# One layer on one core: row sums of w_ada in PSUM, sums at the replacements on VectorE, retention's banks dealt anew, remainders of the weights last

## The chip, the cores and the metric

The kernel runs on one core of one Trainium2 chip. The metric is the device time of one execution in microseconds. A product of two matrices runs on TensorE (PE in the profile), which reads SBUF and writes PSUM. VectorE (DVE), ScalarE (ACT) and GpSimd (POOL) do the elementwise work, and SyncE (SP) issues nearly all DMAs, in the order in which they stand in its queue.

## The reference

One decoder layer with two mixers side by side, 1024 positions, width 2048, 8 + 8 heads of 128:

```python
mod = jax.nn.silu(c) @ w_ada[layer] + b_ada[layer]
shift, scale, gate = jnp.split(mod, 3, axis=-1)
h = rms_norm(x, norm_gain[layer]) * (1.0 + scale[:, None, :]) + shift[:, None, :]
proj = h @ w_in[layer]                                  # 2048 x 8192
...
oa = merge_heads(stick_breaking_attention(qa, ka, split_heads(v_sb, SB_HEADS)))
oa = oa * jax.nn.silu(z_sb.astype(jnp.float32))
...
ob = head_group_norm(chunkwise_retention(qr, kr, vr), ret_norm_gain[layer])
ob = ob * jax.nn.silu(z_r.astype(jnp.float32))
y = jnp.concatenate([oa, ob], axis=-1).astype(x.dtype) @ w_out[layer]
x = x + (gate[:, None, :] * y).astype(x.dtype)
```

All of it is in float32. `w_ada` is 2048 x 6144; only one row vector, silu(c), is multiplied with it.

## The kernel before

**Products.** The two big projections are done by Strassen's scheme in Winograd's form: a *group* yields 256 output columns over half of the inner dimension by seven products (P1 to P7) in place of eight. A product is four pieces of the inner dimension (j = 0 to 3) by three matmuls of 128 x 512: the left operand (the activations: seven combinations A11, S2, S3, A12, S1, A22, S4, each in four tiles) and the weights are each split into a rounded part and a remainder, and hi x hi, hi x lo and lo x hi are added. In the profile `A_h`, `S_h` are left parts, `A_l`, `S_l` their remainders, `wh` the rounded weights (ScalarE, L259), `wl` their remainders (VectorE, L264). `mm3` (L150 to L152) issues the three matmuls of one j one after the other, so a product needs its `wl` with its third matmul. Four *sums* of raw weights for each group (T1 to T4, `make`, L254) run on GpSimd. Results leave PSUM by ScalarE (L286) and VectorE (L292, and L294 with the gate).

**Stages.** 80 groups run in one fixed row on TensorE, 560 products: a (16 groups, named e), b (32, f and g), c (16, h), y (8) and o (8). `plan` lays out at which product and which j each load, sum and split is issued; `run` issues the products. Beside them run tasks that are advanced one step with each *tick*; a tick is one j of a product, three matmuls. All engines' orders are written out by this one loop.

**Replacements.** At the end of a, b, c and y the left operand is replaced, one combination after the other, as soon as its last product is issued: `place` makes the rounded part on ScalarE (L146) and the remainder (L147) on VectorE for j = 0 to 2 and on GpSimd for j = 3. At most one tile is placed in two ticks. At a's end the new left comes from SBUF and GpSimd forms S2 and S4 of it (L682, L685); at the others each tile is loaded from DRAM first (`keep`, `mix`), into one of a few spare tiles (`ld`, `room(5)` lets the first four loads go only while five are spare).

**Beside a**: `second_half` multiplies w_ada's other half: 8 sums, each of 16 tiles of 256 KB with one factor per partition, added up in an SBUF tile (`acc`). For sums 0 to 3 VectorE does all (`weigh`, L436); for 4 to 7 it does half, and ScalarE scales the others (L635), which GpSimd adds (L637). One tile is consumed in two and three ticks in turn; four tiles (`ada_b`) are kept, and the load of the next waits for the oldest (L605, L608). `over_partitions` then sums over partitions by small matmuls (L414), four for each accumulator. `keep_left` also runs there, on GpSimd (L663).

**Beside b and c**: the stick-breaking heads (`sb_heads`: 12 steps per head, `SB_GAP` = 7 ticks apart: `scores` zp, sigmoids, a scan on VectorE, transposes tp, values oT) and then, beside c and y, the retention heads (`ret_heads`: ktp, sp, up, otp). Their PSUM tiles share the banks A0, A1, B and C.

Of the kernel before, what the change touches and what calls it, by code (L numbers as in the profile page):

```python
# [11 lines left out]
F32 = mybir.dt.float32  # L12
# [5 lines left out]
P = 128  # L18
# [11 lines left out]
NP = 4  # L30
# [29 lines left out]
def layer_kernel(ctx, tc, x, c, w_ada, b_ada, norm_gain, w_in, sb_q_gain, sb_k_gain, ret_norm_gain, w_out,  # L60
# [88 lines left out]
    def mm3(o, a_hi, a_lo, b_hi, b_lo, first, last):  # L149
        nc.tensor.matmul(o, a_hi, b_hi, start=first, stop=False, skip_group_check=True)  # L150
        nc.tensor.matmul(o, a_hi, b_lo, start=False, stop=False, skip_group_check=True)  # L151
        nc.tensor.matmul(o, a_lo, b_hi, start=False, stop=last, skip_group_check=True)  # L152
# [81 lines left out]
    class Group:  # L234
# [14 lines left out]
        def make(self, n):  # L249
# [4 lines left out]
            nc.gpsimd.tensor_tensor(t[o], t[a], t[b], op=op)  # L254
# [50 lines left out]
    def plan(groups):  # L305
# [7 lines left out]
        for k, (g, p) in enumerate(flat):  # L313
            g.at[p] = k
        for k, (g, p) in enumerate(flat):
            if p == "P1":
                on(k - 7, 0, lambda g=g: g.load(0))
                on(k - 6, 1, lambda g=g: g.load(1))
                on(k - 3, 1, lambda g=g: g.make("T3"))
                alone = g.at["P6"] == k + 1  # L320
                on(k - 2 if alone else k - 1, 3 if alone else 1, lambda g=g: g.make("T2"))
                on(g.at["P5"] - 3, 0, lambda g=g: g.make("T1"))
                on(max(g.at["P4"] - 4, g.at["P2"] - 1), 1, lambda g=g: g.make("T4"))
# [36 lines left out]
    def run(ks):  # L360

        for k in ks:
# [183 lines left out]
    plan(groups_a + groups_b + groups_c + groups_y + groups_o)  # L546
# [47 lines left out]
    def second_half():  # L594

        order_ = [(i, r) for i in range(8) for r in range(16)]
        src, accs_ = {}, {}
# [12 lines left out]
        def close(i):  # L610
            mod = ps.tile([P, 4], F32, tag="C", name=f"mod_b{i}")
            over_partitions(mod, accs_.pop(i))
# [12 lines left out]
        for n, (i, r) in enumerate(order_):  # L625
            if r == 0:
                accs_[i] = [k1b.tile([P, HALF], F32, tag="acc", bufs=2, name=f"acc_b{i}")]
            t = src.pop((i, r))
            if i < 4 or r % 2 == 0:
                weigh(accs_[i][0], t, r, r == 0)  # L630
            elif r == 1:
                accs_[i].append(k1b.tile([P, HALF], F32, tag="acc2", bufs=2, name=f"acc2_b{i}"))
                nc.scalar.activation(accs_[i][1], t, AF.Copy, scale=silu_c[:, r:r + 1])
            else:
                nc.scalar.activation(t, t, AF.Copy, scale=silu_c[:, r:r + 1])  # L635
                a2 = accs_[i][1]
                at(2, lambda a2=a2, t=t: nc.gpsimd.tensor_tensor(a2, a2, t, op=ALU.add))  # L637
            if r == 15:
                at(10, lambda i=i: close(i))
# [31 lines left out]
    def gather(n):  # L671
# [304 lines left out]
    def sb_heads():  # L976
        vts = {}
        for n in range(NS * NH + TURN + 2):
# [21 lines left out]
            if h < NH:  # L1000
# [6 lines left out]
                if nxt < NH and {f"n{nxt}", f"q{nxt}", f"k{nxt}", f"v{nxt}", f"z{nxt}"} <= ready:  # L1007
# [11 lines left out]
                    elif s == 11 and nxt in early:  # L1019
# [3 lines left out]
                        yield SB_GAP - 2  # L1023
                        continue
            if s == 3 and h < NH:
# [5 lines left out]
                yield SB_GAP - 6  # L1031
# [25 lines left out]
    def ret_heads():  # L1057
# [4 lines left out]
        for h in range(NH):  # L1062
# [47 lines left out]
            def scores_r(g):  # L1110
                sp = ps.tile([P, 4, P], F32, tag=("B", "A1")[g], name=f"sp_{h}_{g}")
# [8 lines left out]
            def values_r(g):  # L1120
# [40 lines left out]
            def finish(g, on, z):  # L1161
                tp = ps.tile([P, HALF], F32, tag=("B", "A0")[g], name=f"otp_{h}_{g}")
# [70 lines left out]
    def take(src, needs=()):  # L1233
# [7 lines left out]
        def tell(n):  # L1241
# [9 lines left out]
            for j in range(NP):  # L1251

                def do(j=j):
                    t = coming.pop((n, j))
                    place(n, j, t, nc.gpsimd if j == 3 else nc.vector)
# [111 lines left out]
```

## Time and profile before

| | |
|---|---|
| median of 3 runs | 2044.01 us (2043.52 to 2044.23) |
| the profiled execution: its own time | 2045.0 us |
| the profiled execution: its span | 2043.1 us |
| mean granted TensorE clock | 0.982 |
| PE busy | 1949.2 us, 95% |
| DVE, ACT, POOL busy | 1414.5 us, 882.9 us, 737.3 us |
| read and written in HBM | 278.51 MB and 108.10 MB, 189 GB/s |

The span runs from the first to the last instruction of the program; 1.9 us of the execution's own time lie around it. Matmuls overlap one another, so the busy time of PE also covers small gaps; what PE loses is seen better in the distances between starts.

### The profile page before, as it was taken

How to read it: one execution, taken by the hardware profiler on the slowest of the kernel's cores; microseconds unless marked ns; L12 is line 12 of the kernel's file. 1: busy time of each engine (PE TensorE's matmuls, PEld its weight loads, DVE VectorE, ACT ScalarE, POOL GpSimd, SP SyncE). 2: the span in 40 equal slices, each digit the busy share in tenths (PEclk: the TensorE clock that was granted, in tenths of full speed). 3: DMA queues.
4: the chain of work that ended last, by engine and by line, in shares of the span. 5: the costliest groups of instructions: out<-in, count | busy, mean ns of one | idle time of the engine just before them, and what ended most of it. 6: DMA issues, size and time to landing. Idle time of an engine off the chain costs nothing. (4 is left out here: it accounts for less than half of the span.)

```text
span 2043.1 us, 26981 instructions
## 1 busy us (share of the span) xinstructions
PE 1949.2 (95%) x9089; PEld 1561.3 (76%) x9089; DVE 1414.5 (69%) x2218; ACT 882.9 (43%) x1598; POOL 737.3 (36%) x507
## 2 busy tenths in 40 slices
PE   5879998998999999999999999899999999999998
PEld 4357777875777777788888888677888887887887
DVE  6668877647557676676666655778787886458655
ACT  4443244454344544545444454544343444345221
POOL 0434478665222223122322322545343444144221
PEclk9879999998999999999999999999999998999999
DMA  9737876633454455443434533867677787457665
GB/s 295 241 114 250 265 261 231 206 98 114 151 189 144 131 171 171 145 139 119 162 104 132 167 107 108 272 212 263 223 245 247 256 290 243 144 165 253 200 203 168
DMA packets 287326, 388.42 MB, mean 190 GB/s; under 512 B 32106, under 2 KB 164276, under 8 KB 287188
## 3 DMA queue, kind: packets, MB, share of 16 engines
q1 hardware_dynamic: 286784, 386.65, 58.5%
q8 instruction: 72, 1.18, 0.2%
q14 instruction: 66, 0.54, 0.1%
q10 hardware_dynamic: 404, 0.05, 0.0%
HBM read 278.51 MB, written 108.10 MB: 189 GB/s over the span
## 5 line engine op out<-in xcount | busy, mean ns | idle before, releaser
L254 POOL TENSOR_TENSOR wr_e<-wr_e,wr_e 128x512 f32<-128x512 f32 x240 | 351.0, 1476 | 746.4 <-DVE wl_e_P L264 679.2
L264 DVE TENSOR_TENSOR wl_e_P<-wr_e,wh_e_P 128x512 fp32r<-128x512 f32 x560 | 494.7, 884 | 119.4 <-ACT wh_e_P L259 119.2
L259 ACT ACTIVATE wh_e_P<-wr_e 128x512 fp32r<-128x512 f32 x560 | 352.0, 630 | 461.7 <-PE b_o L151 56.6
L254 POOL TENSOR_TENSOR wr_e<-wr_e 128x512 f32<-128x512 f32 x80 | 109.4, 1367 | 256.1 <-DVE wl_e_P L264 236.5
L917 DVE TENSOR_TENSOR_SCAN om<-om 128x128 f32<-128x128 f32 (+2 forms) x96 | 111.6, 1163 | 43.7 <-ACT om L908 41.4
L436 DVE SCALAR_TENSOR_TENSOR acc_b<-ada_b,silu_c,acc_b 128x512 f32<-128x512 f32 x88 | 97.9, 1113 | 31.4 <-DMA ada_b<-in_w_ada_dram 30.8
L292 DVE TENSOR_TENSOR pt<-b_f,pt 128x512 f32<-128x512 f32 x64 | 43.9, 687 | 69.3 <-PE b_f L152 69.2
L152 PE MATMUL b_e<-S_h,wl_e_P 128*128 128x512 f32 x192 | 78.7, 410 | 8.9 <-DVE wl_e_P L264 8.7
L150 PE MATMUL b_e<-S_h,wh_e_P 128*128 128x512 f32 x192 | 78.1, 407 | 5.7 <-ACT pt L286 5.7
L908 ACT ACTIVATE om<-zp,rq 128x128 f32<-128x128 f32 (+2 forms) x96 | 56.0, 584 | 61.6 <-PE zp L903 54.0
L151 PE MATMUL b_h<-S_l,wh_e_P 128*128 128x512 f32 x192 | 75.3, 392 | 3.4 <-DVE S_l L147 1.8
L151 PE MATMUL b_e<-S_l,wh_e_P 128*128 128x512 f32 x192 | 77.4, 403 | 0.0
L150 PE MATMUL b_h<-S_h,wh_e_P 128*128 128x512 f32 x192 | 76.7, 400 | 0.5 <-ACT S_h L146 0.5
L964 PE MATMUL oT<-a,v 128*128 128x256 f32 x320 | 76.8, 379 | 0.0
L150 PE MATMUL b_f<-S_h,wh_e_P 128*128 128x512 f32 x192 | 76.5, 399 | 0.0
L152 PE MATMUL b_h<-S_h,wl_e_P 128*128 128x512 f32 x192 | 75.4, 393 | 0.8 <-DVE wl_e_P L264 0.7
L150 PE MATMUL b_g<-S_h,wh_e_P 128*128 128x512 f32 x192 | 75.8, 395 | 0.0
L923 DVE TENSOR_TENSOR be<-be,om 128x127 f32<-128x127 f32 (+2 forms) x96 | 69.9, 728 | 8.0 <-DVE om L917 0.5
L151 PE MATMUL b_f<-S_l,wh_e_P 128*128 128x512 f32 x192 | 75.2, 392 | 0.0
L152 PE MATMUL b_g<-S_h,wl_e_P 128*128 128x512 f32 x192 | 74.9, 390 | 0.0
L152 PE MATMUL b_f<-S_h,wl_e_P 128*128 128x512 f32 x192 | 74.9, 390 | 0.0
L151 PE MATMUL b_g<-S_l,wh_e_P 128*128 128x512 f32 x192 | 74.9, 390 | 0.0
(401 smaller groups left out, 5325.2 us busy)
## 6 DMA issues: line engine op xcount, KB each, us to landing
wr_e<-in_w_in_dram SPq DMA_DIRECT2D x128, 512.0 KB
ada_b<-in_w_ada_dram SPq DMA_DIRECT2D x128, 256.0 KB
part<-pt SPq DMA_DIRECT2D x128, 256.0 KB
pt<-part SPq DMA_DIRECT2D x128, 256.0 KB
fin<-pt SPq DMA_DIRECT2D x128, 256.0 KB
ada_a<-in_w_ada_dram SPq DMA_DIRECT2D x64, 256.0 KB
wr_e<-in_w_out_dram SPq DMA_DIRECT2D x32, 512.0 KB
ld<-fin SPq DMA_DIRECT2D x54, 256.0 KB
```

The source lines that it names most:

```text
L150: nc.tensor.matmul(o, a_hi, b_hi, start=first, stop=False, skip_group_check=True)
L151: nc.tensor.matmul(o, a_hi, b_lo, start=False, stop=False, skip_group_check=True)
L152: nc.tensor.matmul(o, a_lo, b_hi, start=False, stop=last, skip_group_check=True)
L254: nc.gpsimd.tensor_tensor(t[o], t[a], t[b], op=op)
L259: nc.scalar.activation(hi, self.t[RIGHT[p]], AF.Copy)
L264: nc.vector.tensor_tensor(lo, self.t[RIGHT[p]], self.parts[p].bitcast(F32), op=ALU.subtract)
L292: nc.vector.tensor_tensor(t, src, t, op=ALU.add)
L436: nc.vector.scalar_tensor_tensor(acc, src, cj, acc, op0=ALU.mult, op1=ALU.add)
L908: nc.scalar.activation(om[:, :n], zp[:, :n], AF.Sigmoid, scale=rq[:, h, 1, i:i + 1])
L917: nc.vector.tensor_tensor_scan(rev, rev, rev, init, op0=ALU.mult, op1=ALU.bypass)
L923: nc.vector.tensor_tensor(be[:, :m], be[:, :m], om[:, 1:m + 1], op=ALU.mult)
L964: nc.tensor.matmul(ob, v[:, j, :], a[:, cl], start=diag and ib == 0 and b == 0 and j2 == 0, stop=ch == 0 and ib == 2, skip_group_check=True)
```

## The change

Five things, in the order of the file.

- The twelve matmuls of a product are issued by a table in place of `mm3`. `LATE`: first all four j with the rounded weights (hi, then the left's remainder), then all four with the weights' remainder. `FRESH`, for the first product with a combination that has just been placed: j = 0 and 1 in that manner, then j = 2 and 3 as before. The very first product keeps the old order.
- In the stretches around the ends of a, b, c and y (from the last group's P1 to four products behind its P3) the sums T1 to T4 run on VectorE in place of GpSimd.
- `place` uses VectorE for j = 3 too.
- `second_half`: VectorE does all 128 `weigh`s. The accumulator is a PSUM bank (A0 and A1 in turn), copied to SBUF by ScalarE at the end; there is one accumulator for each sum, so the modulation has four small matmuls in all 8 cases.
- Tasks: the gap behind two of the twelve steps of a stick-breaking head is 2 ticks longer. In retention five PSUM tiles get other banks, and both `normal`s stand one tick earlier.

```diff
-    def mm3(o, a_hi, a_lo, b_hi, b_lo, first, last):
-        nc.tensor.matmul(o, a_hi, b_hi, start=first, stop=False, skip_group_check=True)
-        nc.tensor.matmul(o, a_hi, b_lo, start=False, stop=False, skip_group_check=True)
-        nc.tensor.matmul(o, a_lo, b_hi, start=False, stop=last, skip_group_check=True)
+    PARTS = ((0, 0), (0, 1), (1, 0))
+    LATE = [(j, w, x) for j in range(NP) for w, x in PARTS[:2]] + [(j, 1, 0) for j in range(NP)]
+    FRESH = [(j, w, x) for j in (0, 1) for w, x in PARTS[:2]] + [(0, 1, 0), (1, 1, 0)] + \
+        [(j, w, x) for j in (2, 3) for w, x in PARTS]
+    PLAIN = [(j, w, x) for j in range(NP) for w, x in PARTS]
+    fresh = set()
...
         left[n, j] = hi, lo
+        fresh.add(n)
...
-            nc.gpsimd.tensor_tensor(t[o], t[a], t[b], op=op)
+            eng.tensor_tensor(t[o], t[a], t[b], op=op)
...
+        crowded = set()
+        def sum_of(g, n, k, j):
+            on(k, j, lambda: g.make(n, nc.vector if k in crowded else nc.gpsimd))
...
+        for g in lasts:
+            crowded |= set(range(g.at["P1"], g.at["P3"] + 5))
...
-            hi, lo = g.parts.pop(p)
+            o, w, n = getattr(g, into), g.parts.pop(p), LEFT[p]
+            order = PLAIN if not k else FRESH if n in fresh else LATE
+            fresh.discard(n)
             for j in range(NP):
-                a_hi, a_lo = left[LEFT[p], j]
-                mm3(getattr(g, into), hi[:, j, :], lo[:, j, :], a_hi, a_lo, p in ("P1", "P7", "P2") and j == 0,
-                    j == NP - 1)
+                for i in range(3 * j, 3 * j + 3):
+                    q, wi, xi = order[i]
+                    nc.tensor.matmul(o, w[wi][:, q, :], left[n, q][xi], start=p in ("P1", "P7", "P2") and i == 0,
+                                     stop=i == 11, skip_group_check=True)
...
             if r == 0:
-                accs_[i] = [k1b.tile([P, HALF], F32, tag="acc", bufs=2, name=f"acc_b{i}")]
-            t = src.pop((i, r))
-            if i < 4 or r % 2 == 0:
-                weigh(accs_[i][0], t, r, r == 0)
-            elif r == 1:
...
-            else:
-                nc.scalar.activation(t, t, AF.Copy, scale=silu_c[:, r:r + 1])
-                a2 = accs_[i][1]
-                at(2, lambda a2=a2, t=t: nc.gpsimd.tensor_tensor(a2, a2, t, op=ALU.add))
+                acc = ps.tile([P, HALF], F32, tag=f"A{i % 2}", name=f"acc_b{i}")
+            weigh(acc, src.pop((i, r)), r, r == 0)
             if r == 15:
-                at(10, lambda i=i: close(i))
+                total = k1b.tile([P, HALF], F32, tag="acc", bufs=2, name=f"acc_s{i}")
+                at(2, lambda total=total, acc=acc: nc.scalar.activation(total, acc, AF.Copy))
+                at(10, lambda i=i, total=total: close(i, total))
...
-                place(n, j, staged[n, j], nc.gpsimd if j == 3 else nc.vector)
+                place(n, j, staged[n, j])
...
                         split_qk("q", nxt, 1, 2)
-                        yield SB_GAP - 2
+                        yield SB_GAP
...
                 turn_v(vts.pop((h, 1)), sbv[h], 1, "C")
-                yield SB_GAP - 6
+                yield SB_GAP - 4
...
-                tp = ps.tile([P, HALF], F32, tag=("C", "A1")[g], name=f"ktp_{h}_{g}")
+                tp = ps.tile([P, HALF], F32, tag=("C", "B")[g], name=f"ktp_{h}_{g}")
...
-                sp = ps.tile([P, 4, P], F32, tag=("B", "A1")[g], name=f"sp_{h}_{g}")
+                sp = ps.tile([P, 4, P], F32, tag=("A1", "B")[g], name=f"sp_{h}_{g}")
...
-                                  (8, lambda: normal(0)), (10, lambda: normal(1))):
+                                  (7, lambda: normal(0)), (9, lambda: normal(1))):
...
-                tp = ps.tile([P, HALF], F32, tag=("B", "A0")[g], name=f"otp_{h}_{g}")
+                tp = ps.tile([P, HALF], F32, tag=("A0", "A1")[g], name=f"otp_{h}_{g}")
```

Over the whole program VectorE gets 92 instructions more (32 sums, 28 remainders of placed tiles, 32 `weigh`s), GpSimd 88 fewer; SyncE's queue has the same DMAs. Three places show how the rows moved. Line numbers behind the change differ (L150 to L152 become L400, L264 becomes L269, L292 and L294 become L297 and L299, L254 becomes L259, L964 becomes L972).

The first place is TensorE, one ordinary product of group e in the w_ada stretch (a_e, with A12 as `A` and the weights' parts wh and wl). Before:

```order
L150 MATMUL a_e_2695<-A_0_h,wh_e_P_1190 128x512
L151 MATMUL a_e_2695<-A_0_l,wh_e_P_1190 128x512
L152 MATMUL a_e_2695<-A_0_h,wl_e_P_1194 128x512
L150 MATMUL a_e_2695<-A_1_h,wh_e_P_1190 128x512
L151 MATMUL a_e_2695<-A_1_l,wh_e_P_1190 128x512
L152 MATMUL a_e_2695<-A_1_h,wl_e_P_1194 128x512
```

The same product behind the change:

```order
L400 MATMUL a_e_2683<-A_0_h,wh_e_P_1190 128x512
L400 MATMUL a_e_2683<-A_0_l,wh_e_P_1190 128x512
L400 MATMUL a_e_2683<-A_1_h,wh_e_P_1190 128x512
L400 MATMUL a_e_2683<-A_1_l,wh_e_P_1190 128x512
L400 MATMUL a_e_2683<-A_2_h,wh_e_P_1190 128x512
L400 MATMUL a_e_2683<-A_2_l,wh_e_P_1190 128x512
L400 MATMUL a_e_2683<-A_3_h,wh_e_P_1190 128x512
L400 MATMUL a_e_2683<-A_3_l,wh_e_P_1190 128x512
L400 MATMUL a_e_2683<-A_0_h,wl_e_P_1194 128x512
L400 MATMUL a_e_2683<-A_1_h,wl_e_P_1194 128x512
```

The first use of wl moved from the third matmul of the product to the ninth.

The second place is TensorE at the end of b, around the last values of the last stick-breaking head (oT) and the first product of group h (b_h), which is the first with the new A11. Before, oT stands 48 matmuls (four products) ahead of b_h, in front of the product of b_g that uses S2:

```order
L152 MATMUL b_g_9539<-S_3_h,wl_e_P_1270 128x512
L964 MATMUL oT_1_9513<-a_1_0_4648,v_4680 128x256 x2
L964 MATMUL oT_1_9513<-a_3_0_4775,v_4680 128x256 x2
L150 MATMUL b_g_9714<-S_0_h,wh_e_P_1190 128x512
L151 MATMUL b_g_9714<-S_0_l,wh_e_P_1190 128x512
```

Behind the change:

```order
L972 MATMUL oT_1_9577<-a_1_0_4618,v_4650 128x256 x2
L972 MATMUL oT_1_9577<-a_3_0_4753,v_4650 128x256 x2
L400 MATMUL b_h_9818<-A_0_h,wh_e_P_1197 128x512
L400 MATMUL b_h_9818<-A_0_l,wh_e_P_1197 128x512
L400 MATMUL b_h_9818<-A_1_h,wh_e_P_1197 128x512
L400 MATMUL b_h_9818<-A_1_l,wh_e_P_1197 128x512
L400 MATMUL b_h_9818<-A_0_h,wl_e_P_1201 128x512
L400 MATMUL b_h_9818<-A_1_h,wl_e_P_1201 128x512
L400 MATMUL b_h_9818<-A_2_h,wh_e_P_1197 128x512
L400 MATMUL b_h_9818<-A_2_l,wh_e_P_1197 128x512
L400 MATMUL b_h_9818<-A_2_h,wl_e_P_1201 128x512
L400 MATMUL b_h_9818<-A_3_h,wh_e_P_1197 128x512
```

The last oT moved from 48 matmuls ahead of b_h to directly in front of it, and A_3_h, the fourth tile of the new A11, is used by the tenth matmul behind it. On SyncE the load of that tile (`keep_A_3_202`) stands behind the store of what this oT yields (`mix_3_A_272`), before and behind the change; before, one other store stood between the two.

The third place is VectorE at the end of y, from the placing of the last two combinations (A22 as `A`, S4 as `S`) to the remainder of the weights for P4 of group o0 (d_o in the profile). Before:

```order
L147 TENSOR_TENSOR A_2_l<-ld_3777,A_2_h 128x512
L147 TENSOR_TENSOR S_0_l<-ld_3776,S_0_h 128x512
L147 TENSOR_TENSOR S_1_l<-ld_3772,S_1_h 128x512
L147 TENSOR_TENSOR S_2_l<-ld_3773,S_2_h 128x512
L264 TENSOR_TENSOR wl_e_P_1194<-wr_e_1_1187,wh_e_P_1190 128x512
```

Behind the change:

```order
L147 TENSOR_TENSOR A_2_l<-ld_3743,A_2_h 128x512
L147 TENSOR_TENSOR A_3_l<-ld_3742,A_3_h 128x512
L147 TENSOR_TENSOR S_0_l<-ld_3745,S_0_h 128x512
L147 TENSOR_TENSOR S_1_l<-ld_3746,S_1_h 128x512
L147 TENSOR_TENSOR S_2_l<-ld_3744,S_2_h 128x512
L147 TENSOR_TENSOR S_3_l<-ld_3741,S_3_h 128x512
L259 TENSOR_TENSOR wr_e_0_1192<-wr_e_0_1192 128x4x128
L269 TENSOR_TENSOR wl_e_P_1194<-wr_e_1_1187,wh_e_P_1190 128x512
```

Two remainders (A_3_l, S_3_l) and one sum (wr_e) came from GpSimd's row into VectorE's, ahead of wl.

More of the change, by code (lines that the diff above doesn't have):

```diff
@@ L247, in load, with make @@
             self.t[f"B{i + 1}1"], self.t[f"B{i + 1}2"] = r[:, :, 0:P], r[:, :, P:2 * P]
-        def make(self, n):
+        def make(self, n, eng):
             t = self.t
@@ L318, in plan @@
                 on(k - 6, 1, lambda g=g: g.load(1))
[L319 removed]
+                sum_of(g, "T3", k - 3, 1)
                 alone = g.at["P6"] == k + 1
[L321 to L323 removed]
+                sum_of(g, "T2", k - 2 if alone else k - 1, 3 if alone else 1)
+                sum_of(g, "T1", g.at["P5"] - 3, 0)
+                sum_of(g, "T4", max(g.at["P4"] - 4, g.at["P2"] - 1), 1)
             if p in OLD:
@@ L1254, in do @@
                     t = coming.pop((n, j))
-                    place(n, j, t, nc.gpsimd if j == 3 else nc.vector)
+                    place(n, j, t)
                     free(t)
```

12 lines of the change are left out of this document (5 added, 7 removed).

## The prediction

> **What bounds the kernel now.** I read the page's engine shares first, then the stretches, then who TensorE waits for.
>
> ```profile
> PE 1949.2 (95%) x9089; PEld 1561.3 (76%) x9089; DVE 1414.5 (69%) x2218; ACT 882.9 (43%) x1598; POOL 737.3 (36%) x507
> 131.00:396.00 265.00, 251.47 (x1112) 201.78 (x1112) 212.16 (x233) 96.03 (x165) 162.47 (x104) 0.99 0.75 246
> 440.00:504.00 64.00, 54.90 (x213) 40.55 (x212) 48.38 (x51) 31.18 (x56) 37.00 (x24) 0.92 0.37 118
> 1290.00:1337.00 47.00, 40.30 (x166) 29.88 (x165) 38.05 (x43) 23.52 (x41) 26.16 (x19) 1.00 0.86 296
> 1660.00:1706.00 46.00, 41.81 (x195) 33.78 (x194) 38.83 (x76) 23.84 (x48) 22.68 (x16) 0.89 0.72 247
> 1860.00:1892.00 32.00, 28.99 (x121) 23.33 (x120) 28.42 (x36) 16.86 (x30) 15.18 (x10) 0.95 0.81 268
> ...
> 351.95 0.39 PE L150 MATMUL a_e<-A_h,wh_e_P 128*128 128x512 f32 x1
> 352.18 0.39 PE L151 MATMUL a_e<-A_l,wh_e_P 128*128 128x512 f32 x1
> 357.39 0.83 PE L414 MATMUL mod_b<-ones,acc_b 128*128 128x1 f32 x7
> ```
>
> TensorE is the bound, and its row of products is fixed. The table of stretches gives PE, PEld, DVE, ACT and POOL busy (with counts), the granted clock, the DMA share and GB/s. Two neighbouring matmuls start 0.227 us apart, so the counts show what a stretch loses. The w_ada stretch (131 to 396): 1112 matmuls, 96 of them the small L414 ones (0.83 / 7 = 0.12 us each), so 1016 x 0.227 + 11.5 = 242 of 265 us, 23 lost. The end of a (440 to 504): 213 x 0.227 = 48.4 of 64; a few of the matmuls there are the heads' and longer, so I count 14.5 lost. The end of b (1290 to 1337): 166 x 0.227 = 37.7 of 47, 9.3 lost. The end of c (1660 to 1706): some 58 are retention's small ones, taken at 0.12; 137 x 0.227 + 7 = 38 of 46, 8 lost. The end of y (1860 to 1892): 27.5 of 32, 4.5 lost. Together some 59 us.
>
> The waits of PE, in the w_ada stretch and then at the ends of a, b, c and y, name VectorE's weight remainder wl above all (total, times, longest; otp's in the third last line is over the whole span):
>
> ```profile
> PE b_e L152 <- DVE wl_e_P L264: 5.7, 7, 2.1
> PE d_e L152 <- DVE wl_e_P L264: 4.3, 6, 1.2
> PE a_e L152 <- DVE wl_e_P L264: 2.7, 3, 1.6
> ...
> PE b_e L152 <- DVE wl_e_P L264: 4.2, 2, 2.2
> PE b_f L152 <- DVE wl_e_P L264: 4.2, 1, 4.2
> ...
> PE b_h L151 <- POOL S_l L147: 1.5, 2, 0.9
> PE a_h L152 <- DVE wl_e_P L264: 0.9, 1, 0.9
> ...
> PE otp L1164 <- ACT v L757: 1.5, 3, 0.7
> ...
> PE d_y L152 <- DVE wl_e_P L264: 2.2, 1, 2.2
> ...
> PE d_o L152 <- DVE wl_e_P L264: 3.0, 1, 3.0
> ```
>
> Why wl is late: VectorE's groups by form (150 to 330 us, then 1900 to 2000), the spread of one of them, and SyncE's waits:
>
> ```profile
> L436 DVE SCALAR_TENSOR_TENSOR acc_b<-ada_b,silu_c,acc_b 128x512 f32<-128x512 f32 x67 | 73.3, 1094 | 25.9 <-DMA ada_b<-in_w_ada_dram 25.4
> L264 DVE TENSOR_TENSOR wl_e_P<-wr_e,wh_e_P 128x512 fp32r<-128x512 f32 x57 | 60.2, 1056 | 3.5 <-ACT wh_e_P L259 3.4
> L292 DVE TENSOR_TENSOR pt<-d_e,pt 128x512 f32<-128x512 f32 x8 | 5.4, 681 | 0.0
> ...
> L264 DVE TENSOR_TENSOR wl_e_P<-wr_e,wh_e_P 128x512 fp32r<-128x512 f32 x34 | 25.4, 748 | 0.0
> L294 DVE SCALAR_TENSOR_TENSOR ot<-b_o,gate_c,ot 128x512 f32<-128x512 f32 x20 | 15.0, 751 | 26.8 <-PE b_o L152 26.8
> ...
> L436 DVE SCALAR_TENSOR_TENSOR acc_b<-ada_b,silu_c,acc_b x71: 736/753/1792, 149.3 to 342.4; 128x512 f32<-128x512 f32 x71
> ...
> SPq L608 <- POOL acc_b L637: 34.5, 12, 6.6
> ```
>
> With both inputs in SBUF and GpSimd at work a VectorE instruction takes up to 1.79 us, alone 0.74; with one input in PSUM (L292) it stays at 0.68 in the same stretch.
>
> **The change, part by part.**
>
> *w_ada on VectorE, in PSUM.* 128 weighs in place of 96, no scaling on ScalarE, no adds on GpSimd. A weigh that writes PSUM is not in the trace. Its ends are 0.74 (the same form in SBUF, alone) and 1.79 (at its worst); I take 0.75, since only one input is left in SBUF, as with L292, and L294, the same operation out of PSUM, has it. VectorE's rows overlap by some 0.08 (further down three take 1.88 us at 0.68 each), so 0.67 from start to start. The 128 weighs are spread over 2.5 ticks of three matmuls each, 218 us at TensorE's full pace. VectorE then has 128 x 0.67 + 80 wl x 0.8 + 34 adds x 0.61 = 171 us of work in them. The Trainium skill, "SBUF — State Buffer", section "Who interferes with whom", says that a VectorE instruction with at most one SBUF input does not contend with GpSimd, while one with two does; the rows agree (0.68 against up to 1.79). Without that rule, with weighs staying at 1.09, VectorE would have 225 us of work in 218, and the sum below would be 10 us or more smaller.
> SyncE stood 34.5 us behind GpSimd's adds, with weight loads and stores in line behind; that goes. The eight copies to SBUF are hidden: ScalarE is busy for 96 of 265 us. Sums 4 to 7 have four small matmuls less each, two records apiece: 32 x 0.12 = 3.8 us off TensorE.
>
> *wl last.* wl is needed by the ninth matmul instead of the third, 6 x 0.227 = 1.36 us later. Of the 16 waits in w_ada (12.7 us) none is over 2.1, so with VectorE as late as now 1 us would stay; but TensorE runs ahead by what it gains, so some lateness follows. I keep 4 of 12.7, and of the other 6.5 us (restarts, half clock, the waits for L637's sums) a little over 2. Together with the 3.8: **-17** (ends -4, the small matmuls alone, and -22).
>
> *Half clock.* After a long wait the pitch is nearly doubled for a while:
>
> ```profile
> 343.10 0.63 PE L150 MATMUL b_e<-S_h,wh_e_P 128*128 128x512 f32 x1
> 343.52 0.63 PE L151 MATMUL b_e<-S_l,wh_e_P 128*128 128x512 f32 x1
> ```
>
> This 0.42 us stands behind the longest wait for wl in w_ada, 2.1 us. The Trainium skill, "TensorE: Matmul & The Clock Gate", section "Part 1: The HAM clock gate", wants an idle window of about 3.4 us for that. By it waits this short would cost no clock, and the w_ada sum would be some 2 us smaller; the trace shows that they do.
>
> *Replacements.* 7 remainders and 8 sums move from GpSimd to VectorE at each. End of a:
>
> ```profile
> 442.86 0.39 PE L150 MATMUL d_e<-A_h,wh_e_P 128*128 128x512 f32 x1
> 444.72 0.69 DVE L147 TENSOR_TENSOR A_l<-xT,A_h 128x512 fp32r<-128x512 f32 x1 [3.10 <-ACT A_h L146]
> 488.22 1.88 DVE L147 TENSOR_TENSOR S_l<-xT,S_h 128x512 fp32r<-128x512 f32 x3
> 490.03 0.68 DVE L264 TENSOR_TENSOR wl_e_P<-wr_e,wh_e_P 128x512 fp32r<-128x512 f32 x1
> ```
>
> From the first A_l VectorE needed 45 us to that wl. Behind the change 53 instructions stand there, 32 us alone, and eight sums on GpSimd (S2, S4) still collide, 1 us each: 40, so wl ends at 485.5. TensorE without waits would be at the ninth matmul of that product (the 13th behind 442.86) at 442.86 + 13 x 2.72 + 1.8 = 480. Loss 14.5 to 6.5: **-8** (-3 to -11).
> End of y:
>
> ```profile
> 1867.04 1.52 DVE L147 TENSOR_TENSOR A_l<-ld,A_h 128x512 fp32r<-128x512 f32 x1
> 1881.27 0.50 PE L150 MATMUL d_o<-A_h,wh_e_P 128*128 128x512 f32 x1
> 1884.28 0.68 DVE L264 TENSOR_TENSOR wl_e_P<-wr_e,wh_e_P 128x512 fp32r<-128x512 f32 x1
> ```
>
> Here 18 instructions took 17.9 us, with GpSimd at work. Now 26 stand there and GpSimd has nothing: 26 x 0.62 = 16.1, wl at 1883.2, wanted at 1881.27 + 1.82 = 1883.1: **-4** (0 to -4.5). End of c: the same trade, but retention's small instructions stand in between and GpSimd keeps its mixes: **-3** of 8 (+2 to -6).
>
> *Longer gaps.* One head's first step waits for a split k, which now stands two ticks (1.36 us) further ahead; most of 2.41 goes: **-2**.
>
> ```profile
> 766.82 0.39 PE L902 MATMUL zp<-k,q 128*128 128x256 f32 x1 [2.41 <-DVE k L886]
> 1284.47 1.89 PE L964 MATMUL oT<-a,v 128*128 128x256 f32 x8
> 1287.96 0.44 SPq L716 DMA_DIRECT2D ld<-keep_A  x1
> 1292.36 0.62 ACT L146 ACTIVATE A_h<-ld 128x512 fp32r<-128x512 f32 x1
> ```
>
> But the heads end later, and the load of A11's fourth tile stands on SyncE behind the last head's store. From oT's start to A_h's end it took 8.5 us, 8.1 now with one store out of the line. oT stood four products ahead; now the tenth matmul behind it needs the tile, 1.89 + 9 x 0.227 = 3.9 us on. TensorE waits 4.2 us, and some 1.6 of half clock follow. ScalarE's queue behind that A_h holds wh for two products on, wanted only 5 us later. Against this some 2.5 us of wl waits (a_h's 0.9 is the longest) and 1.5 for GpSimd's S_l go: **+2** (-3 to +8).
>
> *Retention's banks, earlier normals:* they bear on otp's three waits, 1.5 us: **-1** (+1 to -2).
>
> Sum: -17 - 8 - 4 - 3 - 2 + 2 - 1 = -33. Against the profiled execution (2045.0, 1.0 over the median) 2012; against the median **2011**.
>
> **The rivals.**
> 1. *Lateness is a rate.* In w_ada VectorE waits 25.4 us for its own loads, with wl in line behind them; a faster TensorE asks for 265 / 248 x 246 = 263 GB/s. Then wl last buys nothing lasting there, 7 of 17: 2021. Against it: 296 GB/s at the end of b.
> 2. *VectorE is full at the replacements.* If half of the 15 moved instructions find GpSimd at work, 1.7 instead of 0.61, each end has 8 us more, and the gains there (15) vanish: 2026.
> 3. *Slower: a weigh into PSUM is dear.* At w us each VectorE has 128 w + 85 us in a stretch that I expect to last some 230. The 33 us are used up and 4 more lost from 128 w + 85 = 267, w = 1.42. At 1.79 it takes 314: 2095. No row shows such a write; against it L292 and L294, 0.68 and 0.75.
> 4. *The late load drags the others along.* If four of the six later combinations come late by the same 4.4 us (1287.96 to 1292.36): 2011 + 18 = 2029.
>
> **How the numbers follow.** My forecast 0.58 (own range 1999 to 2019), rival 1 0.17, rival 2 0.12, rival 3 0.05, rival 4 0.08. 0.2%, 4 us, is about what a measurement here tells from no change. Low end: w_ada -22, the end of a -11, the end of c -6 give 2000, and -3 for the end of b 1995; I take 1996. High end: rivals 2 and 4, 2030; above it only rival 3 and mixtures. Faster: my case, and nearly all of 1, 2 and 4, 0.90; same 0.04; slower 0.06.
>
> **What would show it.** Weighs at about 0.75 us, none near 1.7; waits of PE for wl in w_ada of 4 us or less; that stretch shorter by 17; b_f's wait at the end of a under 3 us, d_o's gone; a new wait of b_h for ScalarE's A_h, 4 us, at the end of b. Weighs above 1.1, waits for ada_b in place of those for wl, or more than 8 us of new waits at the end of b would make it wrong.

## The result, and the profile after

The changed kernel takes 2011.46 us (median of 5 runs, 2008.99 to 2012.43), the kernel before 2043.52 beside it (2040.24 to 2044.23): ratio 0.9844, 95% interval 0.983 to 0.9859. Its profiled execution took 2008.99 us, span 2007.1, mean granted clock 0.984.

The row of products is the same in both kernels, so the two traces can be laid side by side product by product. Here are the stretches of the prediction, cut at the starts of products 14, 86, 104, 122, 346, 437, 460, 500 and 514 (0 to 559). First before, then after: w_ada (14 to 86), the end of a (104 to 122), b with its end (122 to 346), the end of c (437 to 460), the end of y (500 to 514). The columns are from and to, length, then PE, PEld, DVE, ACT and POOL busy, the granted clock, the DMA share and GB/s.

```profile
163.08:393.88 230.80, 217.27 (x962) 173.53 (x960) 184.60 (x199) 84.72 (x145) 151.02 (x97) 0.99 0.77 253
442.86:511.18 68.32, 59.22 (x226) 42.20 (x224) 49.27 (x52) 33.19 (x60) 39.51 (x26) 0.93 0.32 105
511.18:1339.70 828.52, 818.12 (x3769) 652.53 (x3768) 545.85 (x869) 394.33 (x741) 216.52 (x151) 1.00 0.48 152
1641.74:1729.65 87.91, 82.84 (x402) 67.08 (x400) 69.59 (x130) 44.97 (x87) 40.39 (x29) 0.94 0.76 260
1854.07:1898.02 43.95, 40.94 (x177) 33.24 (x176) 38.30 (x47) 22.64 (x39) 20.69 (x15) 0.96 0.72 240
```

```profile
160.40:363.44 203.04, 203.04 (x929) 169.34 (x928) 159.72 (x230) 68.54 (x119) 92.81 (x69) 1.00 0.87 285
412.40:475.45 63.05, 57.23 (x226) 41.40 (x224) 48.78 (x67) 32.98 (x60) 16.48 (x11) 0.95 0.36 114
475.45:1307.56 832.11, 822.98 (x3770) 656.10 (x3769) 537.72 (x884) 389.59 (x741) 189.64 (x136) 0.99 0.48 151
1609.72:1697.44 87.72, 80.81 (x401) 67.09 (x400) 67.85 (x145) 44.74 (x86) 16.91 (x13) 0.94 0.76 257
1821.89:1861.96 40.07, 39.21 (x178) 32.16 (x176) 36.49 (x59) 23.03 (x39) 3.83 (x3) 1.00 0.77 260
```

| stretch | before | after | difference | predicted |
|---|---|---|---|---|
| w_ada | 230.80 | 203.04 | -27.8 | -17 |
| end of a | 68.32 | 63.05 | -5.3 | -8 |
| b with its end | 828.52 | 832.11 | +3.6 | 0 (gaps -2, end +2) |
| end of c | 87.91 | 87.72 | -0.2 | -4 (end -3, banks -1) |
| end of y | 43.95 | 40.07 | -3.9 | -4 |

These make -33.6. The spans differ by 36.0: another 2.7 lie ahead of product 14, which the change hardly touches and which takes from 159.6 to 163.1 us in the fourteen traces; the stretches between these differ by 0.1 in sum. The medians differ by 32, since before's profiled execution lies 1.5 above the median beside it and after's 2.5 below its own.

The engines' shares after, and two of VectorE's groups over the whole span, the remainders and the weighs:

```profile
PE 1930.8 (96%) x9057; PEld 1557.8 (78%) x9057; DVE 1368.8 (68%) x2310; ACT 861.7 (43%) x1574; POOL 584.1 (29%) x419
...
L269 DVE TENSOR_TENSOR wl_e_P<-wr_e,wh_e_P 128x512 fp32r<-128x512 f32 x560 | 449.4, 803 | 130.8 <-ACT wh_e_P L264 127.9
...
L451 DVE SCALAR_TENSOR_TENSOR acc_b<-ada_b,silu_c,acc_b 128x512 f32<-128x512 f32 x120 | 90.0, 750 | 22.2 <-DMA ada_b<-in_w_ada_dram 21.2
```

A weigh into PSUM takes 0.750 us, as assumed, and VectorE has 92 instructions more in 46 us less. In the w_ada stretch nothing is lost any more: its 864 matmuls at 0.227 us and 64 small ones at 0.12 make 204, and each of the eleven kernels of this document that add w_ada's sums up in PSUM takes the same 203.04. The 21 us that VectorE still stands waiting for the tiles of w_ada cost nobody anything. What TensorE still waits for, over the whole span (total, times, longest):

```profile
PE otp L1172 <- ACT be L1158: 6.5, 4, 4.2
...
PE ms L784 <- ACT ld L843: 4.4, 1, 4.4
PE b_h L400 <- ACT A_h L146: 2.9, 1, 2.9
...
PE a_h L400 <- DVE A_l L147: 2.4, 2, 1.7
PE d_y L400 <- DVE wl_e_P L269: 1.9, 1, 1.9
...
PE zp L910 <- DVE k L894: 1.1, 1, 1.1
...
PE d_o L400 <- DVE wl_e_P L269: 0.9, 1, 0.9
...
PE b_f L400 <- DVE wl_e_P L269: 0.5, 1, 0.5
```

No wait for wl is left in w_ada; b_f's went from 4.2 to 0.5, d_o's from 3.0 to 0.9; the new wait of b_h for A_h is there. But two waits grew: `ms` at the end of a, of which nothing was seen before, and `otp` at the end of c, from 1.9 to 4.2. The end of a on three engines (start, duration; a bracket holds the idle time ahead and what ended it):

```profile
449.40 2.49 DVE L147 TENSOR_TENSOR A_l<-xT,A_h 128x512 fp32r<-128x512 f32 x4
451.80 2.49 DVE L147 TENSOR_TENSOR S_l<-xT,S_h 128x512 fp32r<-128x512 f32 x4
454.21 0.68 DVE L269 TENSOR_TENSOR wl_e_P<-wr_e,wh_e_P 128x512 fp32r<-128x512 f32 x1
454.81 0.68 DVE L297 TENSOR_TENSOR pt<-a_f,pt 128x512 f32<-128x512 f32 x1
...
455.53 0.63 ACT L843 ACTIVATE ld<-pt 128x512 f32<-128x512 f32 x1 [5.07 <-DVE pt L297]
...
456.22 1.87 PE L784 MATMUL ms<-ld,mean 128*1 128x512 f32 x2 [4.38 <-ACT ld L843]
```

Read from below: the mean square `ms` waits for ScalarE's square, that for VectorE's add of the result, and that stands behind wl and eight remainders in a row. It is the same queue that b_f's wl came out of late before; TensorE only meets it at another matmul.

### The profile page after: what moved, and what is told of

It reads as the page before. It is cut to its first block, busy times and chain, and to the rows that moved or that the text cites. A ratio compares the mean times of both kernels' runs of the same rounds, so it can differ in the third digit from the quotient of the medians.

```text
span 2007.1 us, 26887 instructions
## 1 busy us (share of the span) xinstructions
PE 1930.8 (96%) x9057; PEld 1557.8 (78%) x9057; DVE 1368.8 (68%) x2310; ACT 861.7 (43%) x1574; POOL 584.1 (29%) x419
## 5 line engine op out<-in xcount | busy, mean ns | idle before, releaser
L259 POOL TENSOR_TENSOR wr_e<-wr_e,wr_e 128x512 f32<-128x512 f32 x216 | 303.4, 1419 | 877.5 <-DVE wl_e_P L269 693.3
L269 DVE TENSOR_TENSOR wl_e_P<-wr_e,wh_e_P 128x512 fp32r<-128x512 f32 x560 | 449.4, 803 | 130.8 <-ACT wh_e_P L264 127.9
L264 ACT ACTIVATE wh_e_P<-wr_e 128x512 fp32r<-128x512 f32 x560 | 351.3, 631 | 343.0 <-PE b_o L400 58.7
L259 POOL TENSOR_TENSOR wr_e<-wr_e 128x512 f32<-128x512 f32 x72 | 93.8, 1303 | 232.6 <-DVE wl_e_P L269 216.4
L925 DVE TENSOR_TENSOR_SCAN om<-om 128x128 f32<-128x128 f32 (+2 forms) x96 | 107.0, 1115 | 64.5 <-ACT om L916 62.6
L451 DVE SCALAR_TENSOR_TENSOR acc_b<-ada_b,silu_c,acc_b 128x512 f32<-128x512 f32 x120 | 90.0, 750 | 22.2 <-DMA ada_b<-in_w_ada_dram 21.2
L297 DVE TENSOR_TENSOR pt<-b_f,pt 128x512 f32<-128x512 f32 x64 | 44.0, 688 | 65.8 <-PE b_f L400 65.8
L400 PE MATMUL b_e<-S_h,wh_e_P 128*128 128x512 f32 x192 | 76.0, 396 | 5.8 <-ACT pt L291 5.7
L291 ACT ACTIVATE pt<-b_e 128x512 f32<-128x512 f32 x48 | 28.7, 599 | 115.8 <-PE b_e L400 115.0
L400 PE MATMUL b_h<-S_h,wh_e_P 128*128 128x512 f32 x192 | 76.1, 397 | 1.0 <-ACT S_h L146 1.0
L400 PE MATMUL b_h<-S_l,wh_e_P 128*128 128x512 f32 x192 | 76.6, 399 | 0.3 <-DVE S_l L147 0.2
L972 PE MATMUL oT<-a,v 128*128 128x256 f32 x320 | 76.8, 379 | 0.0
L400 PE MATMUL b_f<-S_h,wh_e_P 128*128 128x512 f32 x192 | 75.8, 395 | 0.0
L400 PE MATMUL b_g<-S_h,wh_e_P 128*128 128x512 f32 x192 | 75.4, 393 | 0.0
L400 PE MATMUL b_e<-S_l,wh_e_P 128*128 128x512 f32 x192 | 75.4, 393 | 0.0
L400 PE MATMUL b_f<-S_l,wh_e_P 128*128 128x512 f32 x192 | 75.3, 392 | 0.0
L400 PE MATMUL b_g<-S_l,wh_e_P 128*128 128x512 f32 x192 | 75.0, 391 | 0.0
L931 DVE TENSOR_TENSOR be<-be,om 128x127 f32<-128x127 f32 (+2 forms) x96 | 62.5, 651 | 8.1 <-DVE om L925 0.5
L972 PEld LDWEIGHTS oT<-a,v 128*128 128x128 f32 x320 | 60.5, 189 | 9.5
L291 ACT ACTIVATE pt<-b_g 128x512 f32<-128x512 f32 x48 | 28.8, 599 | 87.2 <-PE b_g L400 83.8
L400 PE MATMUL b_h<-S_h,wl_e_P 128*128 128x512 f32 x192 | 56.9, 400 | 0.0
```

The costliest lines, as they stand in the source:

```text
L259: eng.tensor_tensor(t[o], t[a], t[b], op=op)
L264: nc.scalar.activation(hi, self.t[RIGHT[p]], AF.Copy)
L269: nc.vector.tensor_tensor(lo, self.t[RIGHT[p]], self.parts[p].bitcast(F32), op=ALU.subtract)
L291: nc.scalar.activation(t, src, AF.Copy, scale=1.0 if gt is None else gt)
L297: nc.vector.tensor_tensor(t, src, t, op=ALU.add)
L400: nc.tensor.matmul(o, w[wi][:, q, :], left[n, q][xi], start=p in ("P1", "P7", "P2") and i == 0, stop=i == 11, skip_group_check=True)
```

## The experiments

All were run in 5 rounds beside the kernel before, whose median was 2041.9 to 2044.8 in the different sets; so they are compared by their ratio to it (the change: 0.9844). Stretches are of one profiled execution each.

### The order of each product alone

Put into the kernel before, with the same tables:

```diff
-                mm3(getattr(g, into), hi[:, j, :], lo[:, j, :], a_hi, a_lo, ...)
+                for i in range(3 * j, 3 * j + 3):
+                    q, wi, xi = order[i]        # LATE or FRESH
+                    nc.tensor.matmul(o, w[wi][:, q, :], left[n, q][xi], ...)
```

> The kernel before with the new order of each product alone (wl used last; weighs, sums, gaps and banks as before). Theory A (the 16 waits for wl in the w_ada stretch are single ones, none over 2.1 us, and 1.36 us of slack takes nearly all of them): the stretch from 131 to 396 us ends about 10 us earlier, the longest waits at the ends (4.2, 3.0, 2.2) lose 1.36 each with their half clock, some 8 us more: 2026. Theory B (VectorE has 225 us of work for 218 us there, so its lateness comes back as TensorE runs ahead): 3 us in the stretch, the ends as in A, 2033, with waits for wl still in the list inside the stretch.

2044.45 us, ratio 1.0014 (1.0004 to 1.0025): not faster at all, 0.1% slower. The w_ada stretch, and TensorE's waits in it:

```profile
161.24:390.60 229.36, 219.18 (x961) 176.41 (x960) 182.75 (x199) 83.45 (x144) 148.71 (x97) 0.97 0.78 254
```
```profile
PE mod_b L420 <- POOL acc_b L643: 3.9, 3, 1.5
PE b_e L391 <- DVE wl_e_P L267: 2.6, 4, 1.0
PE d_e L391 <- DVE wl_e_P L267: 1.7, 4, 0.6
PE a_e L391 <- DVE wl_e_P L267: 1.2, 2, 0.8
PE b_e L391 <- DVE pt L295: 0.5, 1, 0.5
```

The waits for wl fell from 12.7 to 5.5 us, and the stretch by 1.4. TensorE now waits for the sums of w_ada (3.9) and for an add (0.5) instead, and the granted clock is 0.97 in place of 0.99. At the end of a b_f's 4.2 became a wait of `ms`, 5.4 us, and that stretch has 68.6 us as before. Theory B had the direction; not even its 8 us at the ends came, and the end of y is 2.5 us longer (46.41).

### w_ada's sums in PSUM alone

```diff
-                accs_[i] = [k1b.tile([P, HALF], F32, tag="acc", bufs=2, name=f"acc_b{i}")]
+                acc = ps.tile([P, HALF], F32, tag=f"A{i % 2}", name=f"acc_b{i}")
+            weigh(acc, src.pop((i, r)), r, r == 0)
...
+                at(2, lambda total=total, acc=acc: nc.scalar.activation(total, acc, AF.Copy))
```

> The kernel before with w_ada's sums in PSUM on VectorE alone (plain order of the products). Theory A (weighs at 0.75 us give VectorE 171 us of work for 218, so wl is in time even for the third matmul): nearly the whole of the 23 us lost in the stretch and the 3.8 us of small matmuls are won, 2020. Theory B (more of the stretch's gain belongs to the later use of wl): half of the waits for wl stay, 2031. The difference between this run, the one with the order alone and the whole change says how much the two overlap.

2017.97 us, 0.9886 (0.9871 to 0.9901): Theory A, whose 2020 against 2044 is a ratio of 0.988. The w_ada stretch:

```profile
162.14:365.18 203.04, 203.04 (x930) 169.35 (x928) 161.49 (x230) 69.05 (x120) 93.35 (x69) 1.00 0.87 284
```

It is as long as with the whole change. The weighs account for all of w_ada's 27.8 us, with wl in its old place. (Between the medians lie 23.9 us; the 27.8 are measured against the profiled execution of the kernel before, which is 3 us above its median in this set.)

### The whole change with the plain order

```diff
-            order = PLAIN if not k else FRESH if n in fresh else LATE
+            order = PLAIN
```

> The changed kernel with the plain order of the products (wl by the third matmul). Theory A (the order only matters where VectorE is late: at the ends): w_ada within 3 us of the changed kernel, the ends 1.36 us each and some half clock, 2019. Theory B (in w_ada the slack of 1.36 us is what turns short lateness into none): 10 us more in w_ada alone, 2027.

2011.39 us, 0.9853 (0.9839 to 0.9866): the same as the change. w_ada takes 203.04 again. At the end of a `ms` does not wait; b_f does, for wl:

```profile
PE b_f L400 <- DVE wl_e_P L269: 3.2, 1, 3.2
```

The end of a has 62.1 us here, 63.0 in the changed kernel. So the order moves the wait from one matmul to another and gains nothing that these runs can tell.

### All weighs on VectorE, but in SBUF

```diff
-                acc = ps.tile([P, HALF], F32, tag=f"A{i % 2}", name=f"acc_b{i}")
+                acc = k1b.tile([P, HALF], F32, tag="acc2", bufs=2, name=f"acc_b{i}")
```

> The changed kernel with the 128 weighs accumulated by VectorE in SBUF instead of PSUM (no copy to SBUF is saved; the copy by ScalarE stays). Theory A (it is the second SBUF input that collides with GpSimd, busy 105 of 239 us): weighs average 0.95 us or more, wl slows with them, VectorE has some 215 us of work for 218, and TensorE loses 3 to 10 us: 2017. Theory B (only GpSimd's adds of the partial sums, which are gone here too, collided): weighs at 0.75 to 0.8, the time as the changed kernel's, 2011.

2028.0 us, 0.9935 (0.9923 to 0.9948). The w_ada stretch, the weighs from 150 to 330 us, and their spread:

```profile
161.31:381.90 220.59, 209.43 (x930) 167.63 (x928) 190.56 (x231) 69.08 (x121) 103.88 (x68) 1.00 0.82 264
```
```profile
L451 DVE SCALAR_TENSOR_TENSOR acc_b<-ada_b,silu_c,acc_b 128x512 f32<-128x512 f32 x87 | 92.8, 1066 | 20.2 <-DMA ada_b<-in_w_ada_dram 19.6
```
```profile
L451 DVE SCALAR_TENSOR_TENSOR acc_b<-ada_b,silu_c,acc_b x96: 731/752/1857, 148.7 to 345.0; 128x512 f32<-128x512 f32 x96
```

Theory A, and its loss was larger than stated (17.6 us in the stretch, not 3 to 10). The median weigh is no slower (0.752), but the mean is 1.066, with GpSimd at work for half of the stretch. So of w_ada's 27.8 us 17.6 come from the accumulator's place alone, and 10.2 from the rest together: the additions taken off GpSimd, the scaling off ScalarE, the small matmuls off TensorE, and the new order, which alone was worth 1.4. The rule of the Trainium skill that the prediction cited on this ("SBUF — State Buffer", "Who interferes with whom") holds here.

### The sums and fourth remainders back on GpSimd

```diff
-                place(n, j, staged[n, j])
+                place(n, j, staged[n, j], nc.gpsimd if j == 3 else nc.vector)
...
-    plan(groups_a + ... + groups_o, [gs[-1] for gs in (groups_a, groups_b, groups_c, groups_y)])
+    plan(groups_a + ... + groups_o, [])
```

> The changed kernel with the replacements' sums and fourth remainders back on GpSimd. Theory A (GpSimd's work slows VectorE's there by more than it takes off VectorE): end of a 67 to 68 us in place of 63.0, end of y 43 to 45 in place of 40.1, the end of c within 1 us, the end of b 2 us longer: 2021. Theory B (what the ends won is the later use of wl): ends within 2 us of the changed kernel, 2013.

2024.26 us, 0.9916 (0.9902 to 0.993). The ends of a, b, c and y:

```profile
411.61:479.50 67.89, 57.52 (x225) 40.65 (x224) 49.29 (x52) 32.95 (x60) 39.59 (x26) 0.95 0.33 105
1246.61:1315.71 69.10, 57.54 (x217) 42.92 (x216) 42.76 (x51) 27.89 (x48) 32.70 (x22) 0.90 0.68 221
1616.80:1704.64 87.84, 81.09 (x402) 66.88 (x400) 69.11 (x130) 44.83 (x86) 39.72 (x29) 0.94 0.77 260
1829.08:1875.41 46.33, 42.27 (x177) 34.10 (x176) 40.02 (x47) 22.81 (x39) 21.07 (x15) 0.93 0.68 227
```

Theory A, with more at b and y than it said: the ends of a, b and y are 4.8, 4.1 and 6.3 us longer than in the changed kernel, the end of c is the same. At the end of a VectorE does 15 instructions fewer and is busy for 49.29 us in place of 48.78: taking work off it gained it nothing, since what stayed became slower (0.95 us in place of 0.73 in the mean).

### The stick-breaking heads' gaps

As before the change, and then longer only ahead of the first two heads' successors:

```diff
-                        yield SB_GAP
+                        yield SB_GAP - 2                   # second kernel: SB_GAP - 2 * (nxt > 2)
...
-                yield SB_GAP - 4
+                yield SB_GAP - 6
```

> The changed kernel with the stick-breaking heads' gaps as before. Theory A (the heads end 22 ticks later with the longer gaps, and the load of A11's fourth tile behind them is what TensorE waits for at the end of b): the wait of b_h for ScalarE's A_h (2.9 us) goes, the split k's 2.4 us come back, and the two stretches from product 122 to 346 take 826 us in place of 832: 2006. Theory B (the loss at the end of b is VectorE's, which now has GpSimd's sums and remainders): only the 2.4 us come back, 2014.

2008.47 us, 0.9836 (0.9822 to 0.9851).

> The changed kernel with the longer gap only where a head's last step goes before one of the first two heads' successors (the place of the one 2.4 us wait for a split k), 4 ticks later at the end in place of 22. Theory A: both gains, no wait for k above 1.1 us and no late load: 824 us for products 122 to 346, 2003 to 2005. Theory B: as the changed kernel, 2011.

2000.75 us, 0.9801 (0.9787 to 0.9815): 0.4% below the changed kernel. Products 122 to 346 without the longer gaps, and then with the short form of them:

```profile
478.10:1307.40 829.30, 822.11 (x3769) 655.47 (x3768) 546.92 (x884) 390.72 (x741) 194.85 (x136) 0.99 0.48 152
```
```profile
475.22:1297.68 822.46, 816.95 (x3770) 652.17 (x3768) 528.93 (x884) 391.68 (x741) 187.90 (x136) 1.00 0.48 153
```

The changed kernel has 832.11. In neither of the two does b_h wait for A_h. The split k's waits (3.7 us in six, 2.4 the longest) are back in the first and gone in the second. So the heads' end 18 ticks later cost 9.7 us, and the gap at the one place that needed it gains 6.8, more than the waits themselves: behind the 2.4 us stand 3.4 us at half clock in the first kernel, and another 6.8 at the end of b, which cost 5.1 together and which the second has not. Of the 9.7, too, most is clock in these two executions, as the end of b shows (products 330 to 346, the changed kernel and then the short form):

```profile
1242.57:1307.56 64.99, 56.95 (x218) 43.03 (x217) 45.89 (x66) 28.03 (x48) 9.98 (x7) 0.89 0.69 235
```
```profile
1243.91:1297.68 53.77, 48.32 (x202) 36.85 (x200) 44.14 (x63) 26.72 (x46) 10.19 (x7) 1.00 0.79 277
```

(Some 3 us of the difference are 16 matmuls of the last head, which stand within these products only in the changed kernel.) TensorE's waits there are 7.8 us in sum against 5.4; a granted clock of 0.89 over 65 us is 7.1 us. How much of it is clock differs from one execution to the next: with the plain order, which has the same gaps, the stretch is as long (65.0 us) with 9.9 us of waits and 3.4 lost by the clock.

### Retention's banks and normals as before

```diff
-                tp = ps.tile([P, HALF], F32, tag=("A0", "A1")[g], name=f"otp_{h}_{g}")
+                tp = ps.tile([P, HALF], F32, tag=("B", "A0")[g], name=f"otp_{h}_{g}")
...
-                                  (7, lambda: normal(0)), (9, lambda: normal(1))):
+                                  (8, lambda: normal(0)), (10, lambda: normal(1))):
```

(and likewise `ktp` and `sp`)

> The changed kernel with retention's banks and normals as before. Theory A (with the earlier normals ScalarE's be is queued behind a tile that waits for VectorE, and otp's longest wait grew from 1.9 to 4.2 us by it): that wait falls back to 2 us, the end of c is 2 to 3 us shorter, 2009. Theory B (otp's wait is VectorE's queue, full of the replacement's remainders and sums, wherever the normals stand): end of c 87 to 88 us, 2011 to 2012.

2011.88 us, 0.9855 (0.9839 to 0.987), which can't be told from the change. In the profiled execution, the slowest of its four, otp's longest wait fell to 3.1 us, and still the end of c took longer:

```profile
1610.69:1702.50 91.81, 82.86 (x401) 67.29 (x400) 69.21 (x145) 45.06 (x86) 19.40 (x14) 0.94 0.74 250
```

Two waits for the DMA of the next head's v stand there, 2.6 us in sum. Theory A's wait came out in part (it said 2 us), its gain did not; whether the banks are worth anything stays open.

### The waiting matmuls later

The kernel with the short form of the gaps, and:

```diff
     def mean_square(h, i, hf, sq):
-        yield 4
+        yield 10
...
-            yield RT_GAP
+            yield RT_GAP + 6 * (h == 5)
             finish(0, *o0)
```

> The changed kernel with the longer gap for the first heads only, and the two matmuls that wait longest at the ends put 6 ticks (4 us) later in TensorE's row: the mean squares at the end of a (ms waits 4.4 us for ScalarE's square) and the sixth retention head's otp at the end of c (4.1 us for ScalarE's be). Theory A (what is late is VectorE's queue; ms and otp are only where TensorE meets it, as with wl used later): at the end of a b_f waits some 2.8 us for the wl that stands behind eight remainders (the trace of the changed kernel has it end at 454.9, and the ninth matmul would stand at 452.1), at the end of c the next product waits some 2.8 us for its wl (1663.5 against 1660.7); 1.5 us gained at each, a little half clock, 1997. Theory B (the waits are those two matmuls' own): 4.4 + 4.1 us and about 4 us of half clock behind them, 1988.

2002.83 us, 0.9808 (0.9789 to 0.9826): no gain over that kernel. Over the whole span, and (last three lines) from 1600 to 1720 us:

```profile
PE b_f L400 <- DVE wl_e_P L269: 3.2, 2, 2.7
```
```profile
PE b_y L400 <- DVE wl_e_P L269: 1.4, 1, 1.4
PE b_y L400 <- ACT wh_e_P L264: 1.0, 1, 1.0
PE a_y L400 <- DVE wl_e_P L269: 0.9, 1, 0.9
```

Theory A's wait came at the end of a: b_f waits 2.7 us for wl where `ms` waited 4.4. The gain there was larger than the 1.5 it said: that stretch is 59.65 us in place of 63.25. At the end of c three new waits of 3.3 us together take the place of otp's 4.1, and the stretch is 1 us longer. What was won at a, stage b lost (828.15 in place of 822.46), where all of the mean squares came later; the last experiment tests whether that was the cause.

### Placing faster, placing slower

```diff
-PLACE_GAP = 2
+PLACE_GAP = 1          # second kernel: 3
```

> The changed kernel with the longer gap for the first heads only, and replaced tiles placed one tick apart instead of two. Theory A (VectorE has the same work at each end whatever its order, and TensorE waits for the sum of it): ends of a, b, c and y within 2 us of 63.3, 53.8, 87.6 and 40.1; 2001. Theory B (the remainders now stand in longer rows ahead of each wl, and delay it): ends 2 to 5 us longer each, 2010. Theory C (the work is begun sooner, and VectorE is done sooner): ends 2 to 4 us shorter, 1992.

2010.28 us, 0.9841 (0.9822 to 0.9861).

> The changed kernel with the longer gap for the first heads only, and replaced tiles placed three ticks apart instead of two. Theory A (only VectorE's sum of work counts): as with two, 2001. Theory B (wl stands behind fewer remainders): ends 2 us shorter each, 1993. Theory C (work begun later is late, and the row of remainders that a product needs is longer when it comes): ends 2 to 5 us longer each, 2010.

2006.07 us, 0.982 (0.9802 to 0.9838). Both are slower than two ticks (0.9801 with 0.9787 to 0.9815), one tick by more than the intervals, three within them. From 410 to 480 us, one tick and then three:

```profile
PE b_f L400 <- DVE wl_e_P L269: 4.6, 2, 4.2
```
```profile
PE ms L784 <- ACT ld L843: 4.2, 1, 4.2
PE a_f L400 <- DVE A_l L147: 1.3, 2, 1.1
```

With one tick it is wl that comes late there, with three `ms` still waits 4.2 us and the left parts themselves come late too. In these executions the end of a gained 0.6 and 1.7 us, the ends of b, c and y lost 3.6, 3.3 and 3.8 with one tick (Theory B, but for a), 0.5, 4.2 and 2.4 with three (Theory C at c and y alone).

### Only the first mean square later

```diff
-        yield 4
+        yield 10 if (h, i, hf) == (0, 0, 0) else 4
```

> The changed kernel with the longer gap for the first heads only, and of the mean squares only the first one behind the end of a put 6 ticks later. Theory A (the 3.6 us won at the end of a by the later ms, 59.7 in place of 63.3, are kept, and the 6 us that stage b lost with all mean squares later were lost by the others): 1997. Theory B (what the end of a wins, stage b gives back, since the first head starts later): 2001.

1998.39 us, 0.9774 (0.9761 to 0.9787): the fastest of all, 0.7% below the change; its interval touches that of the kernel with the short gaps alone (0.9787). The end of a:

```profile
414.91:475.59 60.68, 56.57 (x225) 41.17 (x224) 48.77 (x67) 32.75 (x60) 16.48 (x11) 0.97 0.36 118
```

2.6 us less than 63.25, and b keeps its time (823.12): Theory A in these stretches. The profiled execution is the slowest of its five; it is 2.9 us longer than that of the short gaps, all of which lies ahead of product 104.

## Why the prediction was right, step by step

The time was right, 2011.0 against 2011.46, but that it came so near is luck, since two errors cancel: w_ada brought 11 us more than stated, the other four stretches 10 us less.

- **Weighs at 0.75 us, from the row of L294 and the one-input rule:** right, 0.750. The bound without the rule ("10 us or more smaller") held too: with the weighs in SBUF the stretch is 17.6 us longer.
- **w_ada -17:** measured -27.8. The mis-sized step is "I keep 4 of 12.7" with "a little over 2" of the other 6.5. I had worked out 171 us of work in 218 and then still let VectorE be late. With that much room all of it goes: 12.7 of waits for wl, 3.8 of small matmuls, and 11.3 of restarts, half clock and waits for the sums, for which I had written 6.5 although my own 23 less 12.7 leaves 10.3. Nothing of it belongs to "wl last". SyncE's waits behind GpSimd's adds went, as said, but new ones took their place: from 131 to 370 us it waited 73 us for used tiles, all behind VectorE, in place of 103; it cost TensorE nothing.
- **wl last, 1.36 us per wait:** wrong. A wait got shorter, but VectorE's queue did not, and TensorE met it at the next matmul that needed it: at `ms`, the sums, the adds. The order alone gained nothing, and leaving it out lost nothing. Rival 1's remark that it "buys nothing lasting" was right of the order, for VectorE's sake and not the DMA's: the w_ada stretch moved 285 GB/s, more than the 263 of rival 1, and lost nothing. I also counted nine matmuls everywhere: a product with a fresh left part, as d_o at the end of y, needs wl with its fifth.
- **End of a -8:** measured -5.3. VectorE's row was right almost to the tenth (wl done 42.6 us into the stretch by my count, 42.5 in the trace); the wait behind it became `ms`'s, between the sixth and the seventh matmul of that product, 4.4 us and half clock. With the sums and fourth remainders on GpSimd the stretch is 4.8 longer, so its gain is theirs (no run tells the two apart), and rival 2 (a full VectorE) did not come at a, b and y.
- **End of y -4:** measured -3.9, and by the sums again: with them on GpSimd that end has 46.33 us, 2.4 more than before the change.
- **End of c -3, banks -1:** measured -0.2 together. d_y's wait fell only from 2.2 to 1.9, otp's grew to 4.2; the sums' engine makes no difference there.
- **Longer gaps -2, end of b +2:** measured +3.6 for both. The mechanism, the place and the waiter (b_h for ScalarE's A_h) were right, 2.9 us instead of 4.2. The sizes were not: the late end cost 9.7 us instead of 5.8, since the half clock behind it was some 7 us in that execution and not 1.6; and the gap at its one useful place is worth 6.8 instead of 2, again with half clock, of which the kernel before had none behind that wait (last section). Of the 4 us of waits that were to go against it 3.3 went (6.6 before, 3.3 without the longer gaps), but half clock, of which there was none before, took 3.4, and the end of b gained 0.9. The other combinations did not come later by it (a_h's waits are 2.4 us, and 2.9 with the short form), so rival 4 was wrong.

## What to carry to other kernels

A wait names the matmul at which TensorE meets a late engine, not its cause: putting that matmul later shortens the wait and can lengthen the next one. Less work for the late engine, or faster work, took off the most here; a later place paid only for single matmuls (the first mean square, one step of two heads). Ask what each instruction reads from where: an accumulator in PSUM in place of SBUF made 128 instructions 30% cheaper in the mean and was worth more than everything else together (some 18 of 32 us). Where a delay is added for one waiter, add it at that waiter alone and see what stands at the end of the row of delays.

## What the hardware showed that was not expected

- Work moved from GpSimd to VectorE can leave VectorE's busy time where it was: 67 instructions in 48.78 us at the end of a, against 52 in 49.29 with GpSimd at work.
- The length of a wait does not decide alone whether half clock follows. The same wait of 2.41 us for a split k stands in the kernel before (the prediction's row at 766.82) and in the one without the longer gaps (its end at 733.74). Before, no half clock follows; there it does (slices of 3.41 us around the wait, first before, then without the longer gaps; the granted clock is the third number from the end):

```profile
762.36:765.77 3.41, 2.05 (x13) 1.62 (x11) 3.28 (x3) 0.00 (x0) 2.65 (x2) 1.00 0.91 264
765.77:769.19 3.42, 2.37 (x11) 2.04 (x12) 3.23 (x7) 1.15 (x3) 0.00 (x0) 1.00 0.12 40
```
```profile
730.51:733.92 3.41, 1.00 (x8) 0.81 (x7) 3.28 (x5) 0.00 (x0) 1.43 (x1) 1.00 0.65 181
733.92:737.33 3.41, 3.41 (x10) 2.74 (x11) 2.48 (x6) 1.15 (x3) 0.00 (x0) 0.50 0.32 95
```

In each of the fourteen traces half clock begins only at times that lie whole multiples of 3.41 us apart, and lasts whole multiples of it, except where the trace ends (in the changed kernel, behind 150 us, at 454.50, 1263.46, 1280.53, 1297.59 and 1659.40 us, for 6.83, 3.41, 6.83, 3.41 and 10.24). The slices above are cut on that grid. From 150 us on the traces have 60 such slices at full clock in which TensorE stood idle for more than 55%, and all 60 were followed by half clock; of some 7400 with less than 30% one was, of the 81 between them 17. Before the change the 2.41 us are divided over two slices (1.36 and 1.05 idle), without the longer gaps they lie in one. So whether a wait of some 2 us costs a slice at half clock, about 1.7 us, is decided by where it falls, and some of the differences of a few us between single executions above are of this kind.

The Trainium skill, "TensorE: Matmul & The Clock Gate", section "Part 1: The HAM clock gate", calls the window in which activity is counted free-running, which agrees with these rows.
